# Strassen's seven products in eight of eleven column-tile pairs of three SwiGLU up projections

## The chip, the core and the metric

One NeuronCore of a Trainium2 chip runs the whole program. The time is device time in microseconds from start to end of one execution, median of several runs. TensorE (PE) multiplies, loading each matmul's stationary 128x128 operand by a load of its own (PEld); VectorE (DVE), ScalarE (ACT) and GpSimd (POOL) do the elementwise work; SyncE (SP) issues most transfers.

## The reference, cut to what matters

Two transformer blocks in float32 on 512 tokens, width 1024, hidden width 2816. Three SwiGLU layers lie in them: ffn1 at the start, ffn2 at the end of the first block, and a gated one at the end of the second.

```python
def rms_norm(x, g):
    y = x * lax.rsqrt(jnp.mean(x * x, axis=-1, keepdims=True) + EPS)
    return y * g
def swiglu(h, w1, w3, w2):
    return (jax.nn.silu(h @ w1) * (h @ w3)) @ w2
# first block
x = x + 0.5 * swiglu(rms_norm(x, norm_ffn1), ffn1_w1, ffn1_w3, ffn1_w2)
x = x + hybrid_mixer(...)
x = x + memory_attention(...)
x = x + 0.5 * swiglu(rms_norm(x, norm_ffn2), ffn2_w1, ffn2_w3, ffn2_w2)
x = rms_norm(x, norm_out)
# second block: mixing, then
gate, up = jnp.split(rmsnorm(x, g_pre_ffn) @ w_ffn_in, 2, axis=-1)
x = x + rmsnorm((jax.nn.silu(gate) * up) @ w_ffn_down, g_post_ffn)
```

## The kernel before

Activations lie transposed, [width, tokens], in tiles of 128 rows by 512 tokens. Every float32 operand is split in two parts, high (a rounded copy by ACT, L93 or L94) and low (the rest, by DVE, L98 or L99), and each product is three matmuls (`mm3`, L114): high by high, high by low, low by high. All go through L109.

Weights come through `Stream` in an order written out by hand. `next(key)` splits up to four weights beyond the one asked for; SP loads a 512 KB weight tile as soon as one of four `raw` buffers is free. Parts of weights, activations and results share one pool `q` of 41 buffers of 4 KB a partition.

`ffn_up` makes the hidden tiles f = 0 to 21. For each it takes a gate tile and an up tile, each of 8 row chunks (`kk`) by 3 matmuls of 512 tokens, so 48 matmuls a tile. The sum of squares of x is still on its way then: `finish()` gives the row `rb` of 1/rms during tile 1, and `evac` multiplies both results by it (L287, L290), takes silu of the gate (L288), multiplies (L291) and splits the hidden tile at once. `ffn_down` goes through d = 0 to 7, each over all 22 hidden tiles, and adds to the residual x, which stays in SBUF throughout. The third layer begins with two halves of 256 tokens, since its input (`resid2`, L1917) comes half by half; there the matmuls are 256 wide, as in the product before it. Its down product (`ffn_out`) has tokens on the partitions, after 32 transposes of x (L1959).

The order of instructions on each engine is fixed when the program is compiled; tile buffers of a pool are handed out as earlier tiles are released.

Of the kernel before, what the change touches and what calls it, by code (L numbers as in the profile page):

```python
# [36 lines left out]
class Ctx:  # L37
    def __init__(self, ctx, tc, aps):
# [79 lines left out]


class Stream:  # L120
    """Weights in the order of their use: loaded ahead, then split in two exact parts."""

    RAW = 4
    AHEAD = 4

# [42 lines left out]

    def start(self, x, xT, gains):
        """The first two weights come in pieces, between those of x."""  # L170
# [21 lines left out]

    def next(self, key):
        while self.ns <= min(self.n + self.AHEAD, len(self.order) - 1):
            self._split()
# [4 lines left out]


class Norm:
    """Sum over the width of the squares of a transposed residual; then 1/rms by token in two layouts."""
# [1936 lines left out]
```

## Time and profile before

| | |
|---|---|
| median of 3 runs | 2262.35 us (2261.66, 2262.35, 2264.3) |
| span of the profiled execution, from its first to its last instruction | 2260.1 us |
| time of the profiled execution beside its span | not listed apart; the shown runs lie 1.6 to 4.2 us above the span, their median 2.25 |
| instructions | 27814, of them 10730 matmuls |
| busy: PE, PEld, DVE, ACT, POOL | 2229.0, 1846.7, 1261.5, 850.9, 340.9 us |
| up projections, start to end in the span | 6 to 263, 842 to 1065, about 1880 to 2129 us |

Busy time of an engine is the union of its instructions; a matmul's recorded length is longer than its distance to the next. "idle before" in a row is time that the engine stood still ahead of that group, and the name after the arrow is what ended it.

### The profile page before, as it was taken

How to read it: one execution, taken by the hardware profiler on the slowest of the kernel's cores; microseconds unless marked ns; L12 is line 12 of the kernel's file. 1: busy time of each engine (PE TensorE's matmuls, PEld its weight loads, DVE VectorE, ACT ScalarE, POOL GpSimd, SP SyncE). 2: the span in 40 equal slices, each digit the busy share in tenths (PEclk: the TensorE clock that was granted, in tenths of full speed). 3: DMA queues.
4: the chain of work that ended last, by engine and by line, in shares of the span. 5: the costliest groups of instructions: out<-in, count | busy, mean ns of one | idle time of the engine just before them, and what ended most of it. 6: DMA issues, size and time to landing. Idle time of an engine off the chain costs nothing.

```text
span 2260.1 us, 27814 instructions
## 1 busy us (share of the span) xinstructions
PE 2229.0 (99%) x10730; PEld 1846.7 (82%) x10730; DVE 1261.5 (56%) x2063; ACT 850.9 (38%) x1483; POOL 340.9 (15%) x392
## 2 busy tenths in 40 slices
PE   8999999999999999999999999999999999999998
PEld 6888888888888888888888878887777798888887
DVE  7444434556866655444345955736888757544422
ACT  4222223545344523222223543315666643332320
POOL 3000011301233030000230000213334104000000
PEclk9999999999999999999999999999999999999999
DMA  5332324122333322333224132531111451222321
GB/s 173 104 101 94 102 79 137 53 94 80 125 123 103 103 94 98 105 96 96 94 93 147 58 107 93 173 121 58 57 47 57 147 180 57 94 94 94 128 87 38
DMA packets 73292, 224.92 MB, mean 100 GB/s; under 512 B 8388, under 2 KB 11204, under 8 KB 73160
## 3 DMA queue, kind: packets, MB, share of 16 engines
q1 hardware_dynamic: 72584, 222.10, 30.5%
q8 instruction: 84, 1.38, 0.2%
q10 hardware_dynamic: 576, 1.05, 0.1%
q14 instruction: 48, 0.39, 0.1%
HBM read 210.01 MB, written 13.11 MB: 99 GB/s over the span
## 4 chain that ended last, share of the span: by engine, by line
PE 89%; DVE 5%; ACT 2%; issue 2%; POOL 1%; DMA 1%; SPq 0%; DVEq 0%; POOLq 0%; ACTq 0%
PE ps L109 87%; PE ps L112 2%; DVE q L98 1%; ACT q L1456 1%; POOL hr L251 1%; DVE nx L1454 1%; DVE q L99 0%; ACT q L93 0%; DMA q<-in_xT_dram 0%; DVE q L1354 0%; DVE hn L424 0%; POOL q L1461 0%; ACT q L885 0%; DMA raw<-in_w_k_dram 0%; DVE b L428 0%
## 5 line engine op out<-in xcount | busy, mean ns | idle before, releaser
L109 PE MATMUL ps<-q,q 128*128 128x512 f32 (+3 forms) x9744 | 2160.7, 382 | 13.1 <-ACT q L94 6.2
L109 PEld LDWEIGHTS ps<-q,q 128*128 128x128 f32 x9744 | 1743.2, 189 | 349.5 <-issue 6.6
L98 DVE TENSOR_TENSOR q<-raw,q 128x1024 fp32r<-128x1024 f32 (+2 forms) x381 | 471.3, 1260 | 145.1 <-ACT q L93 71.7
L93 ACT CAST q<-raw 128x1024 fp32r<-128x1024 f32 (+2 forms) x381 | 372.1, 1008 | 168.0 <-PE ps L109 90.6
L93 ACT CAST q<-b 128x512 fp32r<-128x512 f32 (+2 forms) x94 | 56.7, 613 | 362.3 <-DVE b L291 316.2
L222 POOL TENSOR_TENSOR b<-q 128x512 f32<-128x512 f32 (+1 forms) x56 | 56.0, 1003 | 764.8 <-DVE q L1651 324.6
L290 DVE TENSOR_TENSOR b<-ps,b 128x512 f32<-128x512 f32 x44 | 30.4, 690 | 163.8 <-PE ps L109 163.8
L98 DVE TENSOR_TENSOR q<-b,q 128x512 fp32r<-128x512 f32 (+2 forms) x94 | 64.6, 695 | 63.6 <-ACT q L93 62.9
L226 POOL TENSOR_TENSOR b<-b,b 128x512 f32<-128x512 f32 (+1 forms) x70 | 95.2, 1365 | 4.2
L1461 POOL TENSOR_SCALAR q<-q,nr 128x128 f32<-128x128 f32 (+3 forms) x128 | 71.9, 568 | 143.4 <-DVE nr L1459 116.2
L1456 ACT ACTIVATE q<-ps,nx 128x128 f32<-128x128 f32 (+3 forms) x128 | 67.4, 531 | 56.2 <-DVE nx L1454 31.0
L94 ACT ACTIVATE q<-q,gains 128x512 fp32r<-128x512 f32 (+1 forms) x48 | 30.3, 650 | 152.4 <-DVE q L1651 71.8
L112 PE MATMUL ps<-ident,q 128*128 128x128 f32 x512 | 80.8, 274 | 3.5 <-POOL q L1461 2.3
L98 DVE TENSOR_TENSOR q<-ps,q 128x512 fp32r<-128x512 f32 x112 | 74.1, 682 | 11.3 <-ACT q L93 10.9
L288 ACT ACTIVATE b<-b 128x512 f32<-128x512 f32 x66 | 41.2, 630 | 102.9 <-DVE b L287 102.8
L112 PEld LDWEIGHTS ps<-ident,q 128*128 128x128 f32 x512 | 61.8, 140 | 20.7 <-POOL q L1461 7.8
L93 ACT CAST q<-ps 128x512 fp32r<-128x512 f32 x112 | 62.7, 593 | 16.7 <-PE ps L109 11.6
L99 DVE SCALAR_TENSOR_TENSOR q<-q,gains,q 128x512 fp32r<-128x512 f32 (+1 forms) x48 | 47.7, 1013 | 17.4 <-ACT q L94 17.4
L1454 DVE TENSOR_REDUCE nx<-ps 128x1 f32<-128x384 f32 (+3 forms) x96 | 56.0, 583 | 0.0
L290 DVE TENSOR_TENSOR b<-ps,rb 128x512 f32<-128x512 f32 x22 | 15.2, 689 | 73.1 <-PE ps L109 73.1
L251 POOL TENSOR_TENSOR sr<-ss,mhalf 128x4 f32<-128x4 f32 x8 | 8.1, 1008 | 297.6 <-DVE ss L1088 192.9
L251 POOL TENSOR_TENSOR or<-ov,mhalf 128x1 f32<-128x1 f32 x4 | 2.2, 547 | 335.5 <-DVE ov L1994 335.5
(244 smaller groups left out, 1118.3 us busy)
## 6 DMA issues: line engine op xcount, KB each, us to landing
raw<-in_ffn_w_dram SPq DMA_DIRECT2D x118, 512.0 KB, 4.0
raw<-in_w_ffn_in_dram SPq DMA_DIRECT2D x44, 512.0 KB, 4.3
raw<-in_w_gm_dram SPq DMA_DIRECT2D x24, 512.0 KB, 3.6
raw<-in_w_ffn_down_dram SPq DMA_DIRECT2D x22, 512.0 KB, 3.6
raw<-in_w_out_dram SPq DMA_DIRECT2D x16, 512.0 KB, 4.2
raw<-in_ffn_w_dram SPq DMA_DIRECT2D x16, 384.0 KB, 3.1
raw<-in_w_mk_dram SPq DMA_DIRECT2D x8, 512.0 KB, 3.8
raw<-in_w_mv_dram SPq DMA_DIRECT2D x8, 512.0 KB, 4.5
```

The lines of the kernel that those rows point to most:

```text
L93: return self.nc.scalar.copy(out, in_)
L98: return self.nc.vector.tensor_sub(out, in_, hi.bitcast(F32))
L99: return self.nc.vector.scalar_tensor_tensor(out, in_, gain, hi.bitcast(F32), op0=ALU.mult, op1=ALU.subtract)
L109: return self.nc.tensor.matmul(out, a, b, start=start, stop=stop)
L112: return self.nc.tensor.transpose(out, in_, self.ident[:n, :n])
L222: k.nc.gpsimd.tensor_tensor(t, x, x, op=ALU.mult)
L226: k.nc.gpsimd.tensor_tensor(self.acc, self.acc, t, op=ALU.add)
L288: nc.scalar.activation(h, h, AF.Silu)
L290: nc.vector.tensor_mul(u, pb, rb)
L1454: nc.vector.tensor_reduce(mx, s.rearrange("p j b t -> p b j t"), axis=AX.XY, op=ALU.max, negate=True)
L1456: nc.scalar.activation(pr[b][:, :n], s[:, :, c, :], AF.Exp, bias=mx[:, c : c + 1], accum_out=sm[:, c : c + 1])
L1461: nc.gpsimd.tensor_scalar(pr[b][:, :n], pr[b][:, :n], r[:, c : c + 1], 1.0, op0=ALU.mult, op1=ALU.mult)
```

## The change

Two neighbouring hidden tiles (columns f = 2n and 2n + 1) make a pair n. With the weight's row chunks taken alternately and the tokens cut in two halves of 256, a pair's product is a product of 2x2 block matrices. For pairs 2 to 5 and 7 to 10 it is made in the seven products of Strassen's scheme (in Winograd's form) instead of eight; pairs 0, 1 and 6 (`PLAIN`) stay as before. Each of the seven is, for gate and up, 4 chunks by 3 matmuls of 256 tokens. Sums and differences of weights are made on DVE from the raw tiles (`_sums`, four for each key), then split; those of the activations once per layer (`Operands.sums`). The results are combined by ACT copies out of PSUM and DVE adds (`take`).

1/rms no longer multiplies the up result: hidden tiles hold silu(gate * rb) * up, unsplit, as halves of a buffer, and are split in the down product. That product is multiplied by rb in ffn1 and ffn2; in the third layer EPS is scaled instead (`e2`). The first four d tiles of the down products of ffn1 and ffn2 run side by side, with their weights laid out anew by the host.

x no longer stays in SBUF during an up projection: it is stored to DRAM (x3d, x6d; ffn1 reads its input again) and loaded back, by transfers issued from ACT. The pool `q` has 39 buffers instead of 41, `raw` 6 instead of 4.

```diff
-        self.qp = pool("q", 41)
+        self.qp = pool("q", 39)
...
+    RAW = 6
...
+    def _sums(self, n):
+        k, nc = self.k, self.k.nc
+        _, _, split = self.order[n]
+        if not isinstance(split, tuple) or split[2] not in ("s12", "s34"):
+            return
+        d, key, what = split
+        if what == "s12":
+            while n >= self.nd:
+                self._dma()
+            d[key].append(self.raw.pop(n))
+        f1, f2 = (t.rearrange("p (k c) -> p k c", c=P) for t in d[key][:2])
+        t = k.q([P, 2, 4, P])
+        eng = nc.vector
+        if what == "s12":
+            eng.tensor_tensor(t[:, 0], f2[:, 0::2], f2[:, 1::2], op=ALU.add)
+            eng.tensor_tensor(t[:, 1], t[:, 0], f1[:, 0::2], op=ALU.subtract)
+        else:
+            eng.tensor_tensor(t[:, 0], f1[:, 0::2], f2[:, 0::2], op=ALU.subtract)
+            eng.tensor_tensor(t[:, 1], f1[:, 1::2], d[key][2][:, 1], op=ALU.subtract)
+        d[key].append(t)
+    def _pair_split(self, n):
+        k = self.k
+        d, key, what = self.order[n][2]
+        if what == "a22":
+            f2 = d[key][1].rearrange("p (k c) -> p k c", c=P)
+            t = k.q([P, 2, 4, P], F32R)
+            k.split(t[:, 0], t[:, 1], f2[:, 1::2])
+            del d[key]
+            return t[:, 0], t[:, 1]
+        t = d[key][2 if what == "s12" else 3].rearrange("p a k c -> p (a k c)")
+        h, l = k.q([P, 1024], F32R), k.q([P, 1024], F32R)
+        k.split(h, l, t)
+        return h, l
...
+    def prefetch(self, ahead):
+        while self.ns <= min(self.n + ahead, len(self.order) - 1):
+            while self.nsum <= min(self.ns + self.SUMS, len(self.order) - 1):
+                self._sums(self.nsum)
+                self.nsum += 1
+            self._split()
...
+class Operands:
+    H = 256
...
+    def add(self, x1, x2, g1, g2, c=slice(0, S), pin=False):
+        k = self.k
+        if c.start == 0:
+            self.b1.append(k.q([P, 2, S], F32R))
+            self.b2.append(k.q([P, 2, S], F32R))
+            self.x.append((x1, x2, g1, g2))
+        j = next(j for j in range(KD // 2) if self.x[j][0] is x1)
+        for b, x, g in ((self.b1[j], x1, g1), (self.b2[j], x2, g2)):
+            k.split(b[:, 0, c], b[:, 1, c], x[:, c], g, pin)
+    def sums(self):
+        k, nc, H = self.k, self.k.nc, self.H
+        for x1, x2, g1, g2 in self.x:
+            z1, z2 = k.b(), k.b()
+            nc.scalar.mul(z1, x1, g1)
+            nc.scalar.mul(z2, x2, g2)
+            t = k.q([P, 4, H])
+            nc.vector.tensor_sub(t[:, 1], z2[:, H:], z1[:, H:])
+            nc.vector.tensor_add(t[:, 0], z1[:, :H], t[:, 1])
+            nc.vector.tensor_sub(t[:, 2:4], z2.rearrange("p (c t) -> p c t", c=2), t[:, 0:1].to_broadcast([P, 2, H]))
+            h, l = k.q([P, 4, H], F32R), k.q([P, 4, H], F32R)
+            k.split(h, l, t)
+            self.th.append(h)
+            self.tl.append(l)
+        self.x = []
...
+PLAIN = (0, 1, 6)
+def up_steps():
+    o, prev = [], None
+    for n in range(NF // 2):
+        rest = [(prev, 4), (prev, 3)] if prev is not None else []
+        if n in PLAIN:
+            o += [(n, "a")] + rest + [(n, "b")]
+        else:
+            o += [(n, 1)] + rest + [(n, 2), (n, 6), (n, 5), (n, 7)]
+        prev = None if n in PLAIN else n
+    return o + ([(prev, 4), (prev, 3)] if prev is not None else [])
+class UpPairs:
+    LEFT = {"a": ("a", 0), "b": ("b", 0), 1: ("f1", 0), 2: ("f1", 1), 3: ("s34", 1), 4: ("a22", 0), 5: ("s12", 0), 6: ("s12", 1), 7: ("s34", 0)}
+    RIGHT = {1: "b11", 2: "b21", 3: "b22", 4: "t4", 5: "t1", 6: "t2", 7: "t3"}
...
+    def product(self, n, num, bank, first, ks=None):
+        k = self.k
+        what, at = self.LEFT[num]
+        ws = self.weights(n, what)
+        for m in range(2):
+            h, l = ws[m]
+            for j in range(KD // 2) if ks is None else ks:
+                if what == "f1":
+                    c = slice((2 * j + at) * P, (2 * j + at + 1) * P)
+                    wh, wl = h[:, c], l[:, c]
+                elif what == "a22":
+                    wh, wl = h[:, j], l[:, j]
+                else:
+                    c = slice((4 * at + j) * P, (4 * at + j + 1) * P)
+                    wh, wl = h[:, c], l[:, c]
+                bh, bl = self.ops.of(self.RIGHT[num], j)
+                k.mm3s(bank[:, m], wh, wl, bh, bl, first and m == 0 and j == 0, j == KD // 2 - 1)
...
+    def out(self, f, half, z, src):
+        k, nc = self.k, self.k.nc
+        c = slice(256 * half, 256 * half + 256)
+        t = k.b([P, 256])
+        nc.vector.tensor_mul(t, src[:, 0], self.rb[:, c])
+        nc.scalar.activation(t, t, AF.Silu)
+        nc.vector.tensor_mul(self.gt(f)[:, c], t, src[:, 1])
...
+    def take(self, n, num):
+        k, nc = self.k, self.k.nc
+        b, c = self.bank, self.c
+        if num in (1, 6, 7):
+            c[n, num] = self.copy(b[n, "x"])
+        if num == 2:
+            z = c.pop((n, 1))
+            nc.vector.tensor_add(z, z, b[n, "z"])
+            c[n, 11] = z
+            del b[n, "z"]
+        if num == 7:
+            z = c.pop((n, 7))
+            nc.vector.tensor_add(z, z, b[n, "y"])
+            self.out(2 * n + 1, 1, z, z)
+        if num == 4:
+            p = b.pop((n, "x"))
+            self.out(2 * n + 1, 0, p, p)
+        if num == 3:
+            z = c.pop((n, 6))
+            nc.vector.tensor_add(z, z, b.pop((n, "y")))
+            self.out(2 * n, 1, z, z)
...
+        for i in range(4):
+            if i == 2:
+                ps += [(k.ps(), w) for w in self.weights(0, "b")]
+            if i in (1, 2):
                 halves = halves()
+            self.plain(*ps[i], slice(0, 256))
+        for p, w in ps:
+            self.plain(p, w, slice(256, 512))
...
+        ps0 = self.first()
+        self.ops.sums()
+        for n, num in steps:
+            if (n, num) == (0, "a") or (n, num) == (0, "b") and early:
+                ps, ps0 = ps0[:2], ps0[2:]
+                pend.append((n, num, ps))
+            elif num in ("a", "b"):
+                ps = [k.ps(), k.ps()]
+                for m, (p, w) in enumerate(zip(ps, self.weights(n, num))):
+                    self.plain(p, w)
+                    if m == 0 and last is None:
+                        last = self.finish()
+                pend.append((n, num, ps))
+            else:
+                first = num in (1, 5, 2)
+                if first:
+                    self.bank[n, which[num]] = k.ps([P, 2, 256])
+                self.product(n, num, self.bank[n, which[num]], first)
+                self.take(n, num)
+            if self.rb is None and last is not None:
+                self.rb = last()
+            if self.rb is not None:
+                while pend:
+                    m, ab, ps = pend.pop(0)
+                    self.out_plain(2 * m + (ab == "b"), *ps)
+                if (n, 11) in self.c:
+                    z = self.c.pop((n, 11))
+                    self.out(2 * n, 0, z, z)
+            if n == NF // 2 - 1:
+                k.W.AHEAD = 2
+                if num == 1:
+                    self.ops.b1 = None
+                if num == 4:
+                    self.ops.th = self.ops.tl = None
+            if num in done:
+                self.w.pop((n, done[num]), None)
+        k.W.AHEAD = Stream.AHEAD
+        return self.g
+def split_g(k, g, f):
+    t = k.q([P, 2, S], F32R)
+    k.split(t[:, 0, :], t[:, 1, :], g[f])
+    g[f] = t
+    ps = [k.ps() for _ in range(4)]
+    for f in range(NF):
+        if f == 0:
+            split_g(k, g, 0)
+        if f + 1 < NF:
+            split_g(k, g, f + 1)
+        if f % 2 == 0:
+            w = k.W.next((key, "a", f // 2))
+        for d in range(4):
+            c = slice((f % 2) * 512 + d * P, (f % 2) * 512 + (d + 1) * P)
+            k.mm3(ps[d], w[0][:, c], w[1][:, c], g[f][:, 0, :], g[f][:, 1, :], f == 0, f == NF - 1)
+    for d in range(4):
+        yield d, ps[d]
+    del ps
+    for d in range(4, KD):
...
+    k.rb = k.const([P, S], "rb")
+    ops, norm = Operands(k), Norm(k)
+    for d in range(0, KD, 2):
+        first[d // 2]()
+        next_pair(x, ops, d, G["norm_ffn1"], norm, True)
+    x.clear()
+    up = UpPairs(k, ("ffn1_w1", "ffn1_w3"), ops, lambda norm=norm: norm.finish(None, k.rb))
+    del ops
+    g = up.run()
     for d in range(KD):
-        if d % 2 == 0:
-            first[d // 2]()
-        next_x(k, x, xs, d, G["norm_ffn1"][:, d : d + 1], norm, True)
-
-    g = ffn_up(k, ("ffn1_w1", "ffn1_w3"), xs, norm.finish)
-    del xs
+        x.append(k.half())
+        nc.scalar.dma_start(x[d], aps["xT"][d])
     xs, norm = [], Norm(k)
     for d, p in ffn_down(k, "ffn1_w2", g):
-        nc.vector.scalar_tensor_tensor(x[d], p, 0.5, x[d], op0=ALU.mult, op1=ALU.add)
+        t = k.b()
+        nc.vector.tensor_mul(t, p, k.rb)
+        nc.vector.scalar_tensor_tensor(x[d], t, 0.5, x[d], op0=ALU.mult, op1=ALU.add)
         next_x(k, x, xs, d, G["norm_mix"][:, d : d + 1], norm)
...
+    ops, norm = Operands(k), Norm(k)
+    x3d = dr.tile([KD, P, S], F32, name="x3d")
     for d, p in out_proj(k, "mo", cat, list(range(KD))):
         nc.vector.tensor_add(x[d], p, x[d])
-        next_x(k, x, xs, d, G["norm_ffn2"][:, d : d + 1], norm)
-
-    g = ffn_up(k, ("ffn2_w1", "ffn2_w3"), xs, norm.finish)
-    del xs
+        if d % 2 == 1:
+            next_pair(x, ops, d - 1, G["norm_ffn2"], norm)
+        nc.scalar.dma_start(x3d[d], x[d])
+    x.clear()
+    up = UpPairs(k, ("ffn2_w1", "ffn2_w3"), ops, lambda norm=norm: norm.finish(None, k.rb))
+    del ops
+    g = up.run()
+    for d in range(KD):
+        x.append(k.half())
+        nc.scalar.dma_start(x[d], x3d[d])
...
+        k.W.AHEAD = min(Stream.AHEAD, KD - 1 - d)
+        ws.append(k.W.next(("wo2", d)))
...
-            k.split(xs[d][:, 0, c], xs[d][:, 1, c], x[d][:, c], G["g_pre_ffn_2"][:, d : d + 1])
+            if d % 2 == 1:
+                g = G["g_pre_ffn_2"]
+                ops.add(x[d - 1], x[d], g[:, d - 1 : d], g[:, d : d + 1], c)
             norm.add(x[d][:, c])
+            nc.scalar.dma_start(x6d[d][:, c], x[d][:, c])
+        if h == 1:
+            x.clear()
...
+        if d > 4:
+            k.W.prefetch(d - 5)
+    k.W.AHEAD = Stream.AHEAD
...
-    g = ffn_up(k, ("gate", "up"), xs, finish, lambda: resid(1))
-    xs.clear()
+    g = UpPairs(k, ("gate", "up"), ops, finish, lambda: resid(1)).run()
+    del ops
     gb = k.q([P, 2, S])
     nc.sync.dma_start(gb, k.a["g_post_rows"])
     xt = []
+    for d in range(KD):
+        x.append(k.half())
+        nc.scalar.dma_start(x[d], x6d[d])
...
+    split_g(k, g, 0)
     for f in range(NF - last):
+        split_g(k, g, f + 1)
         w = k.W.next((key, f))
         for t in range(NT):
             chunk(t, f, w)
+    for f in range(NF - last + 1, NF):
+        split_g(k, g, f)
...
-        nc.vector.scalar_tensor_tensor(v, ss[:, 0:1], EPS, ss[:, 1:2], op0=ALU.add, op1=ALU.add)
+        nc.vector.scalar_tensor_tensor(v, ss[:, 0:1], e2[:, t : t + 1], ss[:, 1:2], op0=ALU.add, op1=ALU.add)
```

## Rows read from the trace of the kernel before

**Rows 1.** Head and part 1 of the profile's page.

```profile
span 2260.1 us, 27814 instructions
...
PE 2229.0 (99%) x10730; PEld 1846.7 (82%) x10730; DVE 1261.5 (56%) x2063; ACT 850.9 (38%) x1483; POOL 340.9 (15%) x392
```

**Rows 2.** Windows: length, then busy of PE, PEld, DVE, ACT, POOL; clock; DMA.

```profile
40.00:263.00 223.00, 223.00 (x987) 184.66 (x986) 108.28 (x130) 69.84 (x89) 0.00 (x0) 1.00 0.29 94
...
386.00:842.00 456.00, 452.55 (x2283) 379.45 (x2283) 291.37 (x552) 201.87 (x350) 109.30 (x101) 1.00 0.31 101
842.00:1065.00 223.00, 223.00 (x990) 184.78 (x989) 107.29 (x130) 69.45 (x89) 0.00 (x0) 1.00 0.29 94
...
1190.00:1866.00 676.00, 670.27 (x3411) 545.55 (x3410) 454.13 (x904) 321.96 (x698) 126.66 (x197) 1.00 0.32 103
...
1922.00:2126.00 204.00, 203.99 (x900) 168.84 (x900) 100.01 (x122) 63.95 (x84) 0.00 (x0) 1.00 0.29 93
```

**Rows 3.** Waits of PE, longest total first: us, times, longest.

```profile
PE ps L109 <- ACT q L94: 6.2, 1, 6.2
PE ps L109 <- DVE q L99: 4.4, 3, 2.6
PE ps L109 <- DVE b L215: 3.6, 1, 3.6
```

**Rows 4.** Groups of instructions in ffn1's up projection, 60 to 240 us.

```profile
L109 PE MATMUL ps<-q,q 128*128 128x512 f32 x795 | 180.4, 389 | 0.0
...
L98 DVE TENSOR_TENSOR q<-raw,q 128x1024 fp32r<-128x1024 f32 x32 | 38.0, 1222 | 5.2 <-ACT q L93 4.3 <-PE ps L109 0.9
L93 ACT CAST q<-raw 128x1024 fp32r<-128x1024 f32 x33 | 33.1, 1045 | 2.1 <-issue 2.1
...
L288 ACT ACTIVATE b<-b 128x512 f32<-128x512 f32 x16 | 10.1, 632 | 33.0 <-DVE b L287 33.0
```

**Rows 5.** Timeline of PE: 256-wide from 1862.60, 512-wide from 1999.75 us (start, length).

```profile
1862.60 20.39 PE L109 MATMUL ps<-q,q 128*128 128x256 f32 x168
1886.55 0.58 PE L109 MATMUL ps<-ones,b 128*128 128x1 f32 x4 [3.56 <-DVE b L215]
...
1999.75 60.45 PE L109 MATMUL ps<-q,q 128*128 128x512 f32 x266
```

**Rows 6.** Windows: 512-wide matmuls in the first stretch, 256-wide in the second.

```profile
60.00:240.00 180.00, 180.00 (x795) 149.05 (x795) 83.04 (x99) 52.01 (x66) 0.00 (x0) 1.00 0.29 93
...
1864.00:1882.00 18.00, 18.00 (x153) 18.00 (x152) 17.21 (x29) 8.41 (x20) 11.43 (x15) 1.00 0.00 1
```

**Rows 7.** Timeline of DVE in the third layer, at four places.

```profile
1864.43 0.76 DVE L1923 TENSOR_TENSOR q<-q,q 128x256 f32<-128x256 f32 x2
...
1905.67 1.39 DVE L99 SCALAR_TENSOR_TENSOR q<-q,gains,q 128x256 fp32r<-128x256 f32 x2 [0.24 <-ACT q L94]
...
1922.52 0.69 DVE L287 TENSOR_TENSOR b<-ps,rb 128x512 f32<-128x512 f32 x1 [5.22 <-ACT rb L263]
1923.13 0.68 DVE L290 TENSOR_TENSOR b<-ps,rb 128x512 f32<-128x512 f32 x1
...
2011.70 0.69 DVE L98 TENSOR_TENSOR q<-b,q 128x512 fp32r<-128x512 f32 x1 [0.74 <-ACT q L93]
2012.65 2.36 DVE L98 TENSOR_TENSOR q<-raw,q 128x1024 fp32r<-128x1024 f32 x2 [0.26 <-ACT q L93]
```

**Rows 8.** Groups by form over the span: 256-wide elementwise work on DVE and ACT.

```profile
L1923 DVE TENSOR_TENSOR q<-q,q 128x256 f32<-128x256 f32 x16 | 7.2, 480 | 0.0
...
L213 ACT ACTIVATE b<-q 128x256 f32<-128x256 f32 x16 | 6.4, 421 | 0.3
```

**Rows 9.** Timeline: transposes behind the third up projection, and a transfer issued from ACT.

```profile
2128.95 3.65 PE L112 MATMUL ps<-ident,q 128*128 128x128 f32 x32
...
2239.64 0.34 ACTq L1999 DMA_DIRECT2D out_dram<-b  x1
```

**Rows 10.** Transfers of x back from DRAM: count, KB each, us to landing.

```profile
q<-x5d SPq DMA_DIRECT2D x8, 256.0 KB, 4.8
```

More of the change, by code (lines that the diff above doesn't have):

```diff
@@ L106, in split, with mm @@
             self.tc.keep_in_program_order(b)
-    def mm(self, out, a, b, start, stop):
-        return self.nc.tensor.matmul(out, a, b, start=start, stop=stop)
+    def mm(self, out, a, b, start, stop, skip=False):
+        return self.nc.tensor.matmul(out, a, b, start=start, stop=stop, skip_group_check=skip)
     def tr(self, out, in_, n=P):
@@ L117, in mm3, with mm3s @@
         self.mm(out, al, bh, False, stop)
+    def mm3s(self, out, ah, al, bh, bl, start, stop):
+        self.mm(out, ah, bh, start, False, True)
+        self.mm(out, ah, bl, False, False, True)
+        self.mm(out, al, bh, False, stop, True)
 class Stream:
-    RAW = 4
+    RAW = 6
     AHEAD = 4
@@ L138, in _dma @@
     def _dma(self):
+        while self.nd < len(self.order) and self.order[self.nd][1] is None:
+            self.nd += 1
         if self.nd < len(self.order):
@@ L147, in _dma @@
             self.raw[self.nd] = t
+            split = self.order[self.nd][2]
+            if isinstance(split, tuple) and split[2] == 0:
+                split[0][split[1]] = [t]
             self.nd += 1
@@ L191, in start @@
                 for d in range(0, KD, 2)]
+    SUMS = 2
     def next(self, key):
[L194 to L195 removed]
+        self.prefetch(self.AHEAD)
         assert self.order[self.n][0] == key, (key, self.order[self.n][0])
@@ L360, in weave, with up_order @@
     return fill
+def up_order(W, keys, srcs):
+    seen = set()
+    for n in range(NF // 2):
+        W.pairs[n, keys] = {}
+    for n, num in up_steps():
+        what = UpPairs.LEFT[num][0]
+        if (n, what) in seen:
+            continue
+        seen.add((n, what))
+        for key, src in zip(keys, srcs):
+            raw = {"f1": lambda: src[2 * n], "s12": lambda: src[2 * n + 1], "a": lambda: src[2 * n],
+                   "b": lambda: src[2 * n + 1]}.get(what, lambda: None)()
+            split = True if what in ("a", "b") else (W.pairs[n, keys], key, 0 if what == "f1" else what)
+            W.order.append(((key, n, what), raw, split))
 def units(k, specs, xs, first=None):
@@ L1893, in second_mix @@
         x.append(t)
-    xs = [k.q([P, 2, S], F32R) for d in range(KD)]
+    ops = Operands(k)
+    x6d = dr.tile([KD, P, S], F32, name="x6d")
     rbf = k.rb
     norms = []
-    ws = [k.W.next(("wo2", d)) for d in range(KD)]
+    e2 = k.const([P, NT], "e2")
+    ws = []
+    for d in range(KD):
+        k.W.AHEAD = min(Stream.AHEAD, KD - 1 - d)
+        ws.append(k.W.next(("wo2", d)))
     halves = (slice(0, 256), slice(256, 512))
@@ L1940, in finish @@
         last = [n.finish(None, rbf[:, c]) for n, c in norms]
+        for n, c in norms:
+            nc.vector.tensor_scalar(e2[:, c.start // P : c.stop // P], n.v, EPS, None, op0=ALU.mult)
         def second():
@@ L1953, in second_mix @@
     xt = []
+    for d in range(KD):
+        x.append(k.half())
+        nc.scalar.dma_start(x[d], x6d[d])
     for t in range(NT):
@@ L1962, in second_mix, with ffn_out @@
     x.clear()
-    ffn_out(k, "down", g, xt, gb, out)
-def ffn_out(k, key, g, xt, gb, out):
+    ffn_out(k, "down", g, xt, gb, e2, out)
+def ffn_out(k, key, g, xt, gb, e2, out):
     nc = k.nc
```

148 lines of the change are left out of this document (88 added, 60 removed).

## The prediction, made before the changed kernel ran

> **What bounds the kernel now.** I read the head of the page first: TensorE is busy for 2229.0 of 2260.1 us, DVE for 56% and ACT for 38% [rows 1]. The windows by stage then say where slack is: in an up projection PE never stops, DVE works 108 of 223 us, ACT 70 and POOL nothing [rows 2]. In the waits of PE the largest are 6.2, 4.4 and 3.6 us, at the start of the kernel and before the third layer [rows 3]. So an up projection is worth what its matmuls take, as long as DVE and ACT keep up; that is the question of this change.
>
> A matmul's recorded length (389 ns in [rows 4]) overlaps the next one's, so the price is the distance between them. 266 of 512 tokens start and end within 60.45 us: less the last one's own 0.39 us, 60.06 / 265 = 226.6 ns. 168 of 256 tokens take 20.39 us; less some 0.29, 20.10 / 167 = 120.4 ns [rows 5]. That is more than half: per column 106.2 / 256 = 0.415 ns, and some 14 ns per matmul whatever its width. At 256 the weight loads are busy 18.00 of 18.00 us, at 512 only 149 of 180 [rows 6].
>
> **The matmuls.** A pair of hidden tiles costs 96 x 226.6 ns = 21.75 us. In seven products it is 7 x 2 keys x 4 chunks x 3 = 168 matmuls of 256, 20.23 us. An eighth of the columns goes, but only 1.52 us (7%) of the time. With 8 pairs in each of 3 layers: 24 x 1.52 = 36.6 us. Every other product keeps its count.
>
> The Trainium skill, "TensorE: Matmul & The Clock Gate", section "Back-to-back issue gap", puts the isolated distance at N / 2.4 + 2.5 ns, so 215.8 and 109.2 ns, and by it the gain would be an estimated 24 x 2.37 = 57 us. The trace doesn't agree: 226.6 and 120.4 ns [rows 5].
>
> **DVE.** Before, it was busy 83 of 180 us [rows 6], or 10.0 us a pair. A pair of seven products wants, over both keys: eight weight sums of 512 elements, low parts of six 1024-wide and two 512-wide tiles, three adds of 512, and eight multiplications of 256 (four quarters of the result, each times rb, then times up). So 13 of 512, 6 of 1024, 8 of 256. Upper price by their recorded lengths, 0.69, 1.222 and 0.48 us [rows 4, 7, 8]: 20.1 us. Back to back they come closer together: 0.61 us from 1922.52 to 1923.13, 2.36 us for two of 1024 less one's 1.22 = 1.14, 0.76 for two of 256 [rows 7]: 13 x 0.61 + 6 x 1.14 + 8 x 0.38 = 17.8 us. PE needs 20.2. DVE goes from less than half busy to 88 to 99%.
>
> To that come waits: each quarter goes DVE, ACT (silu), DVE. A trip to ACT stops DVE for 0.74 us at 512 wide [rows 7]; at 256, with ACT's 0.42 instead of 0.63 [rows 4, 8], some 0.53. Four of them unfilled are 2.1 us: at worst 22.2 us a pair, 2 over PE. At best other weight work fills them and PE stops for nothing. PE's bank x is filled by products 1, 6, 7 and 4 in turn, each after ACT's copy of the one before, with one other product (24 x 0.1204 = 2.9 us) between at the tightest; only a late queue makes that a wait. I take 0.3 us a pair, nearer the low end, because a DVE that is behind has sums and low parts queued that need no silu, and plain pairs 0, 1 and 6 leave it some 10 us each: 24 x 0.3 = 7.2 us (0 to 48).
>
> ACT is not the limit: 6 x 1.05 + 2 x 0.63 + 3 copies + 4 silus come to some 11 us a pair [rows 4, 8].
>
> **Buffers.** In a late pair the pool q holds 16 of operands and 8 to 11 of hidden halves, so of 39 there are 15 to 12 for weights. Step 1 of a pair wants 4 for its own first tile, 4 + 2 of the previous pair's last two products, 4 prefetched and 2 to 4 sums: 16 to 18. In pairs 8, 9 and 10 the prefetch of s12 therefore waits for the previous pair's end and has one product (2.9 us) in which to run; a split is 1.05 + 1.22 us a key [rows 4]. 0 to 2.3 us a pair, I take 0.5, as most of it fits: 9 x 0.5 = 4.5 us (0 to 21).
>
> **The ends of each layer.** `Operands.sums` adds some 11 us of DVE (four times 0.48 + 0.48 + 0.69 + 1.22) and 9 of ACT, once per layer; two plain pairs of 43 us cover it. Without them it would stop PE for most of the 11. At the kernel's start it competes with the low parts that PE already waits for (4.4 us in three waits [rows 3]): 0 to 3, I take 1.
>
> The split of hidden tiles moves to the down product: per tile some 0.63 us of ACT and 0.69 of DVE, with half a weight split, against 12 matmuls or 2.7 us of PE; hidden but for the first tile behind the last quarters. ffn1 and ffn2: 0 to 3 each, I take 1 each. Their eight extra multiplications by rb (0.69 each) lie beside 15 us of matmuls a tile; the 66 removed from the up projections were never waited for.
>
> x: 48 more transfers (24 stores, 16 of them of halves, and 24 loads) are issued from ACT, at 0.34 us each [rows 9] 16 us of its queue in all; behind them stand high parts and silus, and ACT has 9 us spare a pair. A load whose buffer is not yet free holds up that queue. In ffn1 and ffn2 x is wanted only 60 us later. In the third layer 32 transposes (3.65 us, [rows 9]) want all 2 MB directly behind the up projection; one load lands in 4.8 us [rows 10]. 0 if they start when operands are dropped, some 20 us ahead of the end; one after another at half their 4.8 us, some 10. I take 3.
>
> The third layer's second halves are now written tile by tile instead of chunk by chunk. The last low part ends at 1905.67 + 1.39 = 1907.1 us [rows 7], while the first halves end at 1891.8 + 48 x 0.12 = 1897.6: up to 9.5 us in which only the other tiles' chunks could run. I take 2, as the compiled order may still interleave them. Stages outside the layers work with 39 buffers: PE stands idle 3.45 and 5.73 us there now [rows 2]; 0 to 9 more, I take 1.
>
> **Sum.** -36.6 + 7.2 + 4.5 + 1 + 2 + 3 + 2 + 1 = -15.9 us: span 2244.2. The median of the runs lies 2.25 us above the profiled span of before, so 2246 us; with a few us either way in the stalls, 2234 to 2257.
>
> **Rivals.** (1) DVE keeps up entirely and buffers suffice: no stalls, 5 us at the ends; 2260.1 - 36.6 + 5 + 2.25 = 2231. For it: back to back DVE needs 17.8 of 20.2 us. Against: its queue is in fixed order with work for PE mixed with results from PE; the 3.6 us wait for L215 [rows 3, 5] is such a queue at 3.5 us of weight splits.
> (2) DVE sets the pace at some 21.3 us a pair (its recorded lengths and half the silu trips): 24 x 0.45 = 11 us saved, 13.5 lost: 2265, no change to speak of.
> (3) Slower: the silu trips and ACT's high parts stay unfilled, and DVE takes 22.2 us a pair. It decides above 21.75 - 13.5 / 24 = 21.2 us a pair: 24 x 0.45 + 13.5 is 24 us more: 2287.
> (4) Columns alone count: the 14 ns per matmul are not per matmul but a share of the time, and the pair falls to 7/8, 19.03 us: 24 x 2.72 = 65 us saved, 2211. Against: the two widths in the same trace [rows 5]. The skill's gap above, by 2.5 ns a matmul, leans to this side with 2219.
>
> **How the numbers follow.** Chances: the forecast 0.48, (1) 0.17, (2) 0.14, (3) 0.17, (4) 0.04. A measurement of this kernel tells about 0.2% (4.5 us) from no change. Faster than 2257.8: the forecast, (1), (4) and 0.03 of (2), 0.72; within 0.2%: 0.08 of (2); slower: the rest of (2) and (3), 0.20. The range 2222 to 2272 leaves out (4) and most of (3), some 0.16.
>
> **What would show it.** Right: a pair's steps 20.2 to 21 us apart in the timeline, matmuls of 256 at 120 ns, DVE 85 to 97% busy in the up windows, PE's waits there below 4 us a layer for weights (L98) and copies. Wrong: PE waiting over 1 us a pair for DVE or ACT (rival 2 or 3), waits bunched in pairs 8 to 10 (buffers), a gap ahead of the transposes (x), or a distance other than 120 ns.

## The result, and the profile after

The changed kernel takes 2250.61 us (median of four, 2249.97 to 2252.38) against 2262.01 for the kernel before on the same chip: a ratio of 0.9949 [0.9935, 0.9963]. That is faster by 11.4 us where the forecast said 16; the time lies 4.6 us above the forecast, inside its own range of 2234 to 2257. The profiled execution took 2252.38 us, 1.8 more than its span; it is the slowest of the four, so a difference of spans shows some 2 us less won than the medians (9.5 against 11.4).

Head and part 1 of the changed kernel's page, which answer to [rows 1]:

```profile
span 2250.6 us, 31999 instructions
...
PE 2202.8 (98%) x12458; PEld 1905.5 (85%) x12458; DVE 1499.6 (67%) x2517; ACT 998.0 (44%) x1733; POOL 345.1 (15%) x392
```

PE works 26.2 us less than before, and the span falls by only 9.5: PE stands idle for 47.8 us instead of 31.1. Where the idle time lies is read from places that both kernels pass. First PE's timeline of the kernel before (start, length), at places that [rows 5] and [rows 9] do not show:

```profile
40.00 345.71 PE L109 MATMUL ps<-q,q 128*128 128x512 f32 x1524
385.55 0.95 PE L109 MATMUL ps<-ones,b 128*128 128x1 f32 x8
...
842.65 7.53 PE L109 MATMUL ps<-q,q 128*128 128x512 f32 x32
...
1191.34 2.05 PE L109 MATMUL ps<-b,ones 128*128 128x128 f32 x16 [0.45 <-DVE b L258]
...
1922.09 3.25 PE L109 MATMUL ps<-q,q 128*128 128x512 f32 x13
...
2132.36 8.00 PE L109 MATMUL ps<-q,q 128*128 128x512 f32 x34
```

And PE's timeline of the changed kernel:

```profile
39.78 199.35 PE L109 MATMUL ps<-q,q 128*128 128x512 f32 x1488
239.80 6.95 PE L109 MATMUL ps<-q,q 128*128 128x256 f32 x52 [0.68 <-ACT b L455]
247.21 127.25 PE L109 MATMUL ps<-q,q 128*128 128x512 f32 x560 [0.45 <-DVE q L98]
374.30 0.95 PE L109 MATMUL ps<-ones,b 128*128 128x1 f32 x8
...
835.29 15.02 PE L109 MATMUL ps<-q,q 128*128 128x512 f32 x65
...
1172.93 2.05 PE L109 MATMUL ps<-b,ones 128*128 128x128 f32 x16 [0.45 <-DVE b L325]
...
1862.33 0.50 PE L109 MATMUL ps<-q,q 128*128 128x256 f32 x2 [0.67 <-ACT q L93]
1863.59 2.89 PE L109 MATMUL ps<-q,q 128*128 128x256 f32 x22 [0.76 <-DVE q L98]
1870.05 0.98 PE L109 MATMUL ps<-ones,b 128*128 128x1 f32 x4 [3.58 <-DVE b L282]
...
1884.38 0.62 PE L109 MATMUL ps<-q,q 128*128 128x256 f32 x3 [0.97 <-DVE q L99]
1885.65 0.90 PE L109 MATMUL ps<-q,q 128*128 128x256 f32 x3 [0.65 <-DVE q L99]
1888.01 18.21 PE L109 MATMUL ps<-q,q 128*128 128x256 f32 x107 [1.45 <-DVE q L99]
...
1913.53 11.66 PE L109 MATMUL ps<-q,q 128*128 128x512 f32 x52
...
2108.57 0.49 PE L112 MATMUL ps<-ident,q 128*128 128x128 f32 x3
2114.03 5.48 PE L112 MATMUL ps<-ident,q 128*128 128x128 f32 x28 [4.97 <-DMA q<-x6d]
2121.89 18.46 PE L109 MATMUL ps<-q,q 128*128 128x512 f32 x73 [2.37 <-ACT q L93]
```

Subtract place by place (a group's name is that of its first instruction: the first line of the changed kernel holds 256-wide matmuls too). The lead over the kernel before grows, shrinks and grows again:

| place, before → after | lead, us | what the stretch up to it gave |
|---|---|---|
| first up projection at full pace, 40.00 → 39.78 | 0.2 | 0.2 |
| end of ffn1, 385.55 → 374.30 | 11.3 | 11.0 won |
| start of ffn2's up projection, 842.65 → 835.29 | 7.4 | 3.9 lost, in the mixing between |
| end of ffn2, 1191.34 → 1172.93 | 18.4 | 11.1 won |
| first halves of the third layer done, 1886.55 [rows 5] → 1870.05 | 16.5 | 1.9 lost |
| third up projection at full pace, 1922.09 → 1913.53 | 8.6 | 7.9 lost |
| its end, transposes, 2128.95 [rows 9] → 2108.57 | 20.4 | 11.8 won |
| first matmul of the down product, 2132.36 → 2121.89 | 10.5 | 9.9 lost |
| end of the span | 9.5 | 1.0 lost |

Three layers win 11 to 12 us each, and 24.6 us go again at the seams between stages, above all in three of them. In the pairs, but for each layer's last, nothing waits. Windows of the changed kernel (length; busy PE, PEld, DVE, ACT, POOL; granted clock; DMA), the first of them inside ffn1's pairs, answering to [rows 6]; the rest are for later:

```profile
70.00:130.00 60.00, 60.00 (x502) 60.00 (x502) 53.41 (x81) 30.13 (x46) 0.00 (x0) 1.00 0.33 106
...
1870.00:1876.00 6.00, 5.95 (x28) 5.98 (x29) 3.88 (x6) 1.13 (x2) 1.63 (x1) 0.50 0.97 352
...
1888.00:1894.00 6.00, 5.99 (x29) 5.73 (x30) 5.03 (x9) 3.38 (x7) 4.35 (x6) 0.55 0.19 66
...
2109.00:2122.00 13.00, 5.66 (x30) 5.39 (x30) 1.68 (x5) 5.39 (x11) 0.00 (x0) 0.74 0.37 132
```

502 matmuls in 60.00 us are 119.5 ns each, DVE is 89% busy and PE does not stop. ACT's copies of one product start at 71.07, 91.16, 111.32 and 131.48 us in successive pairs, so a pair takes 20.1 us. PE's first stop in that projection is the 0.68 us at 239.80, in the last pair. The 0.45 us at 247.21 are already the down product's: of the group of 52 ahead of them only 48 belong to the pair's last two products.

### The profile page after: what moved, and what is told of

Same layout as the page of the kernel before. It is cut to its first block, busy times and chain, and to the rows that moved or that the text cites. A ratio compares the mean times of both kernels' runs of the same rounds, so it can differ in the third digit from the quotient of the medians.

```text
span 2250.6 us, 31999 instructions
## 1 busy us (share of the span) xinstructions
PE 2202.8 (98%) x12458; PEld 1905.5 (85%) x12458; DVE 1499.6 (67%) x2517; ACT 998.0 (44%) x1733; POOL 345.1 (15%) x392
## 4 chain that ended last, share of the span: by engine, by line
PE 88%; DVE 6%; issue 2%; ACT 2%; POOL 1%; DMA 1%; SPq 0%; DVEq 0%; POOLq 0%; ACTq 0%
PE ps L109 85%; PE ps L112 2%; DVE q L98 1%; ACT q L1743 1%; DVE nx L1741 1%; POOL hr L318 1%; DVE q L99 1%; ACT q L93 0%; DVE q L2229 0%; DVE q L2230 0%; DMA raw<-in_ffn_w_dram 0%; DMA q<-x6d 0%; DMA q<-in_xT_dram 0%; DVE hn L711 0%; DVE nr L1745 0%
## 5 line engine op out<-in xcount | busy, mean ns | idle before, releaser
L109 PE MATMUL ps<-q,q 128*128 128x512 f32 (+2 forms) x11472 | 2131.3, 347 | 23.1 <-DVE q L99 8.5
L109 PEld LDWEIGHTS ps<-q,q 128*128 128x128 f32 x11472 | 1799.2, 191 | 273.9 <-DVE q L99 12.2
L98 DVE TENSOR_TENSOR q<-raw,q 128x1024 fp32r<-128x1024 f32 (+3 forms) x379 | 438.9, 1176 | 99.6 <-ACT q L93 48.7
L93 ACT CAST q<-raw 128x1024 fp32r<-128x1024 f32 (+3 forms) x379 | 352.0, 957 | 120.6 <-PE ps L109 86.4
L98 DVE TENSOR_TENSOR q<-q,q 128x1024 fp32r<-128x1024 f32 (+1 forms) x176 | 175.0, 1014 | 72.5 <-ACT q L93 64.2
L93 ACT CAST q<-q 128x1024 fp32r<-128x1024 f32 (+1 forms) x176 | 152.3, 883 | 137.3 <-PE ps L109 76.3
L464 ACT ACTIVATE b<-b 128x256 f32<-128x256 f32 x96 | 39.9, 417 | 138.6 <-DVE b L463 138.6
L112 PE MATMUL ps<-ident,q 128*128 128x128 f32 x512 | 83.5, 281 | 11.1 <-DMA q<-x6d 5.0
L455 ACT COPY b<-ps 128x512 f32<-128x512 f32 x72 | 42.0, 584 | 94.5 <-PE ps L109 94.5
L93 ACT CAST q<-ps 128x512 fp32r<-128x512 f32 x112 | 62.7, 593 | 16.9 <-PE ps L109 11.6
L465 DVE TENSOR_TENSOR q<-b,b 128x256 f32<-128x256 f32 x72 | 30.1, 423 | 17.3 <-ACT b L464 17.0
```

Of the source, the lines that this page charges most:

```text
L93: return self.nc.scalar.copy(out, in_)
L98: return self.nc.vector.tensor_sub(out, in_, hi.bitcast(F32))
L112: return self.nc.tensor.transpose(out, in_, self.ident[:n, :n])
L455: self.k.nc.scalar.copy(z, bank)
L464: nc.scalar.activation(t, t, AF.Silu)
```

## Experiments: the price of a matmul and DVE's room

**A kernel before with narrow matmuls (narrow_plain).** Every tile behind the first (in the third layer behind the first two) in two passes over 256 tokens: the same columns, 2976 matmuls more.

```diff
-            product([m])
+            product([m], slice(0, 256))
+            product([m], slice(256, 512))
```

> The kernel before, with each gate or up tile from the second on made in two passes of 256 tokens instead of one of 512: the same columns, twice the matmuls. If a matmul costs some 14 ns beside its columns, as 226.6 and 120.4 ns say, a tile costs 48 x 0.1204 - 24 x 0.2266 = 0.34 us more, and 124 tiles 42 us: 2304 us. If columns alone count (rival 4 of the prediction), nothing: 2262 us.

2299.7 us, ratio 1.0165 [1.0151, 1.0179]: 37.5 us more where 42 were expected, or 12.6 ns for each added matmul. PE's timeline of this kernel:

```profile
59.81 190.36 PE L109 MATMUL ps<-q,q 128*128 128x256 f32 x1585
```

(190.36 - 0.28) / 1584 is 120.0 ns from one to the next, and 2 x 120.0 - 226.6 = 13.4 ns is what a cut costs. With no Strassen, no sums and no pool changed, the fixed price per matmul stands between these two widths; rival 4 (columns alone) falls. Whether the price is the matmul's or that of its weight load these runs do not tell: each added matmul brings a load, and at 256 the loads are busy all the time.

**The weight sums done twice (sums_twice).**

```diff
+            for _ in range(2):
                 eng.tensor_tensor(t[:, 0], f2[:, 0::2], f2[:, 1::2], op=ALU.add)
                 eng.tensor_tensor(t[:, 1], t[:, 0], f1[:, 0::2], op=ALU.subtract)
```

(and the two subtractions of the other sums likewise)

> The changed kernel, with each weight sum computed twice into the same tile: eight VectorE additions of 0.685 us more in every Strassen pair, 5.5 us, and nothing else. Reading of the traces: VectorE was busy some 18 us of a pair's 20.2, hidden with about 2 us to spare, so 5.5 more make it the engine that sets the pace: 23.4 us a pair, less what the buffers and pairs 1 and 6 give back, 50 to 80 us over 24 pairs: 2300 to 2330. Rival (VectorE has far more room than its busy time says, or its sums run ahead through the plain pairs): under 10 us more, below 2260.

2285.88 us, ratio 1.0108 [1.0093, 1.0123]: 35 us more than the changed kernel, so DVE became the bound, though it is 14 us less than my lower figure and far above the rival's 2260. The window of ffn1's pairs, and PE's longest waits in ffn1's up projection:

```profile
70.00:130.00 60.00, 58.78 (x476) 58.37 (x475) 56.98 (x91) 26.75 (x41) 0.00 (x0) 0.97 0.27 87
```

```profile
PE ps L109 <- ACT b L457: 7.6, 5, 2.1
```

DVE is at 95%, and PE waits. It waits for ACT by name, though ACT works 26.75 of 60 us: the only edit is on DVE, and ACT itself waits there 26.8 us for DVE (23.4 in the changed kernel), with its copies and high parts in one queue with the silus and splits. So 5.5 us of additions a pair cost 35.3 / 24 = 1.5, and 4.0 were taken in. That is more than the 2.2 us that DVE's busy share leaves of a pair's 20.2; that the plain pairs give the rest is likely, but no run shows it.

**The weight sums on GpSimd (sums_pool).** `eng = nc.vector` becomes `eng = nc.gpsimd`.

> The changed kernel with the eight weight sums of a pair on GpSimd in place of VectorE. Reading: TensorE never waited for VectorE in the steady pairs, so taking 5.5 of its 18 us away is worth nothing: 2247 to 2254, if GpSimd's additions (1.1 to 1.4 us each for such a tile by other rows, 9 to 11 us of a pair) come early enough. Rival 1: VectorE's load costs at the ends of the layers, and the time falls by 5 us or more, to 2245 or less. Rival 2: the slower sums arrive late for the splits, and the pairs wait: 2260 or more.

2271.78 us, ratio 1.0043 [1.0028, 1.0058]: 21 us more than the changed kernel. The time is the second rival's; its reason, sums that come late for the splits, shows little: in ffn1's up projection ACT's splits waited 4.1 us for POOL's sums, in two waits. From the timeline of that kernel (start, length): two multiplications of one shape on DVE, and POOL's sums.

```profile
87.56 0.41 DVE L463 TENSOR_TENSOR b<-b,rb 128x256 f32<-128x256 f32 x1
...
91.05 2.74 POOL L207 TENSOR_TENSOR q<-raw 128x512 f32<-128x512 f32 x2 [11.96 <-PE ps L109]
...
93.16 0.91 DVE L463 TENSOR_TENSOR b<-b,rb 128x256 f32<-128x256 f32 x1
93.74 2.92 POOL L208 TENSOR_TENSOR q<-q,raw 128x512 f32<-128x512 f32 x2
```

And its groups by form, 70 to 130 us:

```profile
L98 DVE TENSOR_TENSOR q<-raw,q 128x1024 fp32r<-128x1024 f32 x6 | 12.4, 2105 | 0.0
```

The multiplication takes 0.41 us with POOL at rest and 0.91 beside POOL's addition; a low part takes 2.105 us instead of 1.222 [rows 4]. Work taken from DVE made DVE's remaining work slower; how the 21 us divide between that and late sums is open. A test of DVE's room by relief was therefore spoilt; sums_twice and the next kernel carry that point.

**Nine pairs (nine_pairs).** `PLAIN = (0, 1, 6)` becomes `(0, 1)`.

> The changed kernel with pair 6 made by Strassen too, nine pairs of eleven in each layer. Reading: TensorE sets the pace in the pairs, and one more saves what the others saved, 1.4 to 1.5 us a pair by the first two layers: 2245.5 to 2247. Rival: the plain pair 6 is where VectorE and the buffers catch up; without it waits of TensorE appear in pairs 8 to 10 of each layer, and the time is 2250 or more.

2245.26 us, ratio 0.9931 [0.9914, 0.9947]: 5.4 us less than the changed kernel, 1.8 a pair, slightly more than expected. In all three up projections PE's waits are the changed kernel's, in ffn1's 0.7 and 0.4 us. Nine Strassen pairs in a row bring no new wait: the plain pair 6 was not needed for catching up.

## Experiments: the four places that lost

**The third layer's second halves, chunk by chunk (halves_by_chunk).** In `UpPairs.first`:

```diff
-        for p, w in ps:
-            self.plain(p, w, slice(256, 512))
+        for kk in range(KD):
+            for p, w in ps:
+                self.plain(p, w, slice(256, 512), [kk])
```

> The changed kernel, with the third layer's second halves made chunk by chunk over its four tiles, as before the change. Theory: the order by tile makes PE wait for the last low part (0.97, 0.65 and 1.45 us) and costs it the full clock behind that; 5 to 8 us less than the changed kernel: 2243 to 2246 us. Rival: the loss there is that of the waits ahead of it, for weights and for the sum of squares (0.67, 0.76 and 3.58 us, then half the clock); then this order brings 2 us at most.

2246.27 us, ratio 0.993 [0.9918, 0.9943]: 4.3 us less than the changed kernel, a little short of the theory's 5 and above the rival's 2. PE's timeline:

```profile
1868.12 0.98 PE L109 MATMUL ps<-ones,b 128*128 128x1 f32 x4 [3.57 <-DVE b L282]
...
1889.68 8.49 PE L109 MATMUL ps<-q,q 128*128 128x256 f32 x47 [0.32 <-DVE q L99]
...
1907.66 7.55 PE L109 MATMUL ps<-q,q 128*128 128x512 f32 x32 [1.62 <-ACT rb L330]
```

From the first halves to full pace it is 39.5 us, against 43.5 in the changed kernel and 35.5 in the kernel before. Three waits of 0.97, 0.65 and 1.45 us become one of 0.32; a new one of 1.62 for the row rb shows up, since PE now comes there early. The stretch in front of the second halves stays slow: behind the wait of 3.57 us PE needs 6.5 us until they begin (1868.12 to 1874.58; in the changed kernel 1870.05 to 1876.59), against 5.3 in the kernel before (1886.55 to 1891.80).

**x loaded by SyncE (x_by_sync).**

```diff
-        nc.scalar.dma_start(x[d], x6d[d])
+        nc.sync.dma_start(x[d], x6d[d])
```

> The changed kernel, with the eight loads of x ahead of the last down product issued from SyncE instead of ScalarE. Theory: on ScalarE they stand behind copies that wait for PE, and the transposes wait 4.97 us for them, with half the clock behind it; on SyncE they start some 10 us sooner: 7 to 10 us less, 2241 to 2244 us, and no wait of PE for x6d. Rival: they wait for buffers of the pool and start no sooner, or hold back the weights of the down product that SyncE loads: no change, the wait moves to other weights.

2243.96 us, ratio 0.992 [0.9908, 0.9933]: 6.7 us less, where 7 to 10 were expected. In the changed kernel, ACT's timeline (ACTq lines are transfers that it issues) shows why:

```profile
2092.12 0.33 ACTq L2273 DMA_DIRECT2D q<-x6d  x1
...
2102.07 0.59 ACT L455 COPY b<-ps 128x512 f32<-128x512 f32 x1 [5.17 <-PE ps L109]
...
2103.88 0.33 ACTq L2273 DMA_DIRECT2D q<-x6d  x1
...
2110.24 0.81 ACTq L2273 DMA_DIRECT2D q<-x6d  x2
```

Between the first and the second load ACT stood 5.17 us for PE ahead of a copy, then waited for DVE ahead of the silus, and each load stood behind them in its order; the last two go out 1.2 us after PE had come to the transposes. With the loads on SyncE's queue the first goes out at 2089.37 and the other seven from 2096.24 to 2100.57. PE's timeline:

```profile
2107.23 3.54 PE L112 MATMUL ps<-ident,q 128*128 128x128 f32 x31
2113.60 16.61 PE L109 MATMUL ps<-q,q 128*128 128x512 f32 x65 [2.83 <-ACT q L93]
```

The 4.97 us gap is gone and the transposes take 3.54 us, close to [rows 9]; the wait behind them, for the first split of g (the hidden tiles), stays. From the first of them to the down product it is 6.4 us, against 13.3 in the changed kernel and 3.4 before: x cost 6.9 us there, and 3.0 are left.

**Both (both).** The two edits together.

> Both of these edits. Theory: they are at different places and add up: 12 to 17 us less than the changed kernel, 2234 to 2238 us. Rival: one of them brings nothing, or the compiled order elsewhere shifts and eats it.

2241.38 us, ratio 0.9908 [0.9894, 0.9921]: 9.2 us less than the changed kernel, where the single edits give 4.3 and 6.7; below the 12 to 17 that I expected. The waits for rb and for the split of g are in neither edit; the difference to 11.0, the sum of the single gains, lies within the intervals.

**And the split of g ahead of the transposes (ends).** `split_g(k, g, 0)` moves from `ffn_out` to the line ahead of the loads of x.

> Both mends (loads of x on SyncE's queue, second halves chunk by chunk), and the first split of g for the down product of the third layer written ahead of the transposes, so that ScalarE does it before the eight copies of transposed rows. Reading: with both mends TensorE still waited 2.84 us behind the transposes for that split; nothing else is late there, so 2238 to 2239.5, against 2241.4 for both mends. Rival: another operand is late behind it (the first down weights' splits, which stand behind the same copies), and it stays at 2240 to 2242.

2237.43 us, ratio 0.9894 [0.9879, 0.9909]. PE's timeline has no gap any more behind the transposes:

```profile
2105.19 3.55 PE L112 MATMUL ps<-ident,q 128*128 128x128 f32 x31
2108.49 21.82 PE L109 MATMUL ps<-q,q 128*128 128x512 f32 x95
```

That is 4.0 us less than with both edits. Three edits at the ends of the third layer give back 13.2 us by the medians and 14.5 by the spans (2236.1 here), of the 20.7 that the spans lost there.

**The buffers alone, in the kernel before (before_39, before_q39).** The first has `q` 39 and `RAW = 6`, the second `q` 39 and `RAW = 4`.

> The kernel before with the buffers of the changed one alone: 39 large ones in place of 41, and six in place of four for weights that arrive. The changed kernel lost about 4 us in the differential attention, beginning with a wait of 2.48 us for VectorE's rc. If the two buffers fewer cause it, this kernel shows the same wait and 3 to 6 us more than the kernel before: 2265 to 2268. Rival: the order of work that the up projection hands on causes it: within 2 us of the kernel before.

> The kernel before with 39 large buffers in place of 41, its four for arriving weights kept. If the two large buffers fewer put the 2.48 us wait into the differential attention, it is here as with 39 and six: 2263.5 to 2266. If the two more for arriving weights do (splits that run ahead fill the large ones earlier), the wait is gone and the time is the kernel before's within 1 us.

2264.81 us, ratio 1.0011 [1.0001, 1.002], and 2266.47, ratio 1.0021 [1.0012, 1.0031]: 2.9 and 4.8 us more, the one at the edge of its expected range and the other 0.5 us above it. PE's timeline of the second:

```profile
440.62 37.34 PE L109 MATMUL ps<-q,q 128*128 128x512 f32 x168
480.44 0.30 PE L112 MATMUL ps<-ident,q 128*128 128x128 f32 x1 [2.48 <-DVE rc L552]
```

That is the changed kernel's wait, without a line of Strassen:

```profile
468.90 0.30 PE L112 MATMUL ps<-ident,q 128*128 128x128 f32 x1 [2.48 <-DVE rc L839]
```

In the kernel before, 162 matmuls stand ahead of this transpose and it does not wait:

```profile
440.33 35.97 PE L109 MATMUL ps<-q,q 128*128 128x512 f32 x162
476.14 0.27 PE L112 MATMUL ps<-ident,q 128*128 128x128 f32 x1
```

With two large buffers fewer the attention's work is compiled in another order: in the changed kernel DVE stands 4.04 us ahead of the softmax at 466.24 for scores from PE. From the end of ffn1 (385.55) to the matmul with ones behind the attention (682.66 in the kernel before) PE needs 4.4 us more in the first kernel, 2.9 in the second and 4.4 in the changed one, which wins 0.5 again until ffn2. Both edits have the wait, so six arriving weights neither cause nor cure it.

**The best of all (ends_nine, ends_nine_q40).** ends with nine pairs; then `q` 40 and `RAW = 5`.

> The same and pair 6 by Strassen too. Reading: the pairs are TensorE's, so the 5.3 us that nine pairs gave alone come on top: 5 to 6 us less than the kernel without them, 2232.5 to 2234.5. Rival: part of that had come from the third layer's end, which is mended here: 2 to 4 us less.

> The same with 40 large buffers and five for weights that arrive, in place of 39 and six. Reading: too few large buffers cost the differential attention its 2.48 us wait and the half clock behind it, so one more takes part of it back: 0 to 4 us less than with 39, if 40 are enough, and five arriving weights are enough for the pairs (a pair takes four). Rival: with five a weight arrives late in each pair, VectorE and TensorE wait, and the time is 10 us or more longer.

2232.75 us, ratio 0.9872 [0.9855, 0.9888], and 2231.14, ratio 0.9867 [0.9853, 0.9882]. Nine pairs give 4.7 us here, a little under the 5 to 6 expected. With 40 buffers PE's timeline is that of the kernel before again, 162 matmuls and no wait:

```profile
427.94 35.97 PE L109 MATMUL ps<-q,q 128*128 128x512 f32 x162
463.75 0.27 PE L112 MATMUL ps<-ident,q 128*128 128x128 f32 x1
```

The time falls by 1.6 us, which the intervals do not tell from nothing; PE waits for high parts (L93) 3.9 us in all there. This last kernel is 30.5 us faster than the kernel before.

## Why the prediction was right, and where its sum was not

The direction and the mechanism held: PE's matmuls set the pace, an eighth fewer columns give 7% of a pair, and DVE keeps up. By terms, in us:

| term of the sum | predicted | measured, and where |
|---|---|---|
| matmuls of 24 pairs | -36.6 | -36.7, as a remainder: 33.9 won in the three layers, and 2.8 of waits in them |
| steady stalls behind DVE | +7.2 | 0 |
| late pairs' buffers | +4.5 | +1.9, the last pair's 0.68 in ffn1 and in ffn2 and 0.56 in the third, by another cause |
| kernel start, down starts | +3 | +0.7: -0.2 at the start, 0.45 among the first matmuls of ffn1's and of ffn2's down product |
| third layer's x | +3 | +6.9 of the 9.9 around the transposes |
| first split of g in the third layer, and the rest until the end | not in the sum | +3.0 of the 9.9, and 1.0 |
| third layer's second halves | +2 | +7.9, and 1.9 in the first halves |
| 39 buffers elsewhere | +1 | +3.9: 4.4 in the differential attention, less 0.5 behind it |
| sum | -15.9 | -9.5, the span's |

- **Matmuls.** The step from [rows 5] to 14 ns a matmul was right at 256 and 512, 119.5 ns in the pairs and 13.4 by narrow_plain, and a pair took 20.1 us, just under the 20.2 to 21 that I had named. "Whatever its width" was wrong: from the first transpose at 2128.95 [rows 9] to the down product at 2132.36, 32 matmuls of 128 columns lie 106.6 ns apart, where 0.415 ns a column and 14 give 67. By that row, which is one of transposes, a 128-wide matmul would cost nearly what a 256-wide one does (an estimate). The Trainium skill, "TensorE: Matmul & The Clock Gate", section "Back-to-back issue gap", has 2.5 ns for an isolated matmul, and by it narrow_plain would have cost an estimated 2976 x 2.5 ns = 7.4 us. It cost 37.5: the trace does not agree.
- **DVE.** The 88 to 99% came out as 89%, but "0.3 us a pair" was mis-sized: it was nothing. The trips to ACT were not all filled: in 70 to 130 us 6 of 12 stopped DVE, for 2.9 us in all. But DVE, back to back as priced, worked only 17.9 us of a pair's 20.1, so these stops did not reach PE, as rival 1 had it, and sums_twice took in 4.0 us more a pair. Rivals 2 and 3 had their condition, DVE behind PE, only where the sums were doubled.
- **Late pairs.** The bunching in pairs 8 to 10 that the buffers were to bring is not there. The waits came in the last pair alone, and nine pairs do not lengthen them. The prediction had "one other product" between ACT's copy and the next use of bank x "at the tightest"; in the last pair there is none, since `up_steps` puts product 4 right behind 7 there, where in other pairs the next pair's product 1 lies between. ACT's and DVE's timeline of the changed kernel:

```profile
239.16 0.59 ACT L455 COPY b<-ps 128x512 f32<-128x512 f32 x1 [1.73 <-PE ps L109]
...
246.47 0.69 DVE L98 TENSOR_TENSOR q<-q,q 128x512 fp32r<-128x512 f32 x1
```

PE ends product 7 at 239.13, ACT copies until 239.75, and PE goes on at 239.80. No run changes that order. The second line is the low part of the first hidden tile, for which PE waits 0.45 us at 247.21: the cost of the down start that the prediction put at 1.
- **x.** I set 3 us, between 0 "if they start when operands are dropped" and some 10. (That bound does not follow from its words: eight loads at half of 4.8 us are 19.) The gap ahead of the transposes that I had named as a sign of being wrong is there, and x cost 6.9 us, by a way that the prediction named (a load holds up ACT's queue) turned round: ACT's own work, waiting for PE and DVE, held up the loads.
- **The first split of g.** I priced the split that moved to the down product for ffn1 and ffn2 only. In the third layer it cost 3.0 us by the starts in x_by_sync, and ends, which moves it forward, gives 4.0.
- **Second halves.** "The compiled order may still interleave them" was the failed step: it did not. 9.5 us was the bound and 7.9 came, of which 6.6 lie in the second halves and 1.3 in front of them, behind the wait for the sum of squares; a kernel without the change lost as much there (before_q39, in the last section). halves_by_chunk takes back 3.9 (43.5 to 39.5 us). Of the 4.0 left 1.2 lie in front of the second halves, 0.6 in them and 2.2 behind them, 1.6 of these the wait for rb.
- **39 buffers.** The sign was right and the size low: 4.4 us in one place, and before_39 loses the same 4.4 there.

Rival 1 (2231) was right for the pairs and wrong for the ends; that the forecast came as near the time as it did is in part luck, since errors of opposite sign made up for part of each other: 9.8 us too much for stalls in the pairs and 2.3 for the starts, against 18.6 too little for x, the split of g, the second halves and the buffers (24.6 instead of 6). With three edits at the seams, eight pairs came to 2237.4.

Open: the waits of 0.67 and 0.76 us before the first halves end, and how the 21 us of sums_pool divide.

## What to carry to other kernels

A scheme that trades columns for more, narrower matmuls is to be priced by the measured distance of both widths, not by columns: here 7/8 of the columns cost 93% of the time, and the price of the two widths does not hold for a third. When its steady part has been costed, most of what remains lies at the seams: a load in the queue of an engine that itself waits for the stage, a loop order that asks for late operands one tile at a time, a split written behind other work of its engine, and two buffers taken from a stage that is elsewhere. All were found by subtracting start times at common places, and the first three were mended by a few lines.

## What the runs showed of the hardware

**GpSimd and VectorE.** A 128x256 multiplication on DVE took 0.41 us alone and 0.91 beside a GpSimd addition, and low parts of 1024 went from 1.222 to 2.105 us (sums_pool). The Trainium skill, "SBUF — State Buffer", section "SBUF: two separate sides", says that a DVE operation with two operands in SBUF and a GpSimd operation that reads SBUF take turns at one pair of ports, each for a whole instruction. The rows agree that the two slow each other (the multiplication and the low part both read two operands in SBUF); that the turn is a whole instruction they do not show.

**The clock behind a short wait.** Behind the 3.58 us at 1870.05 the granted clock was 0.50 over the next 6 us, that is the lower of 1.2 and 2.4 GHz, and behind 0.97 + 0.65 + 1.45 us it was 0.55; around the transposes 0.74 over 13 us. In the kernel before, the 3.56 us in [rows 5] were followed by this, in its windows:

```profile
1886.00:1892.00 6.00, 5.45 (x33) 5.48 (x34) 3.41 (x7) 1.93 (x2) 1.63 (x1) 0.72 0.87 319
1892.00:1898.00 6.00, 6.00 (x53) 6.00 (x52) 5.51 (x11) 1.80 (x4) 3.24 (x5) 1.00 0.29 98
```

A wait alone does not decide it. In before_q39, whose source is the same there, the same 3.56 us were followed by 0.50 over 6 us, and PE needed 6.1 us where the kernel before needs 4.9 (1889.79 to 1895.90, 1886.55 to 1891.44). In the differential attention it is the other way round: the wait of 2.47 us in before_39 was followed by the lower clock, and that of 2.48 us in before_q39 by the full one; windows of the first and the second:

```profile
481.00:484.00 3.00, 3.00 (x10) 2.22 (x9) 2.84 (x9) 2.79 (x8) 0.00 (x0) 0.50 0.00 0
```

```profile
481.00:484.00 3.00, 3.00 (x17) 2.43 (x15) 2.85 (x7) 2.94 (x9) 0.00 (x0) 1.00 0.00 0
```

10 against 17 matmuls in the same 3 us. So a wait of 2 to 4 us may cost its length alone or some microseconds at half the clock as well; these runs do not say beforehand which.
